# A GELU between two matmuls: half of a loaded in whole rows and turned ahead of the first matmuls

## The chip, the cores and the metric

The kernel runs on one core of a Trainium2 chip. The metric is the device time in microseconds (us) of one execution. Five engines work side by side: TensorE (PE in the profile; its weight loads are PEld), VectorE (DVE), ScalarE (ACT), GpSimd (POOL) and SyncE (SP). SP, ACT and GpSimd can issue transfers (DMAs), and 16 DMA engines carry them out.

## The reference

```
m, k, n, p = 1024, 1024, 2048, 1024        # a: m x k, b: k x n, c: n x p, all float32
h = np.matmul(a, b)
h = 0.5 * h * (1 + np.tanh(np.sqrt(2 / np.pi) * (h + 0.044715 * h ** 3)))
return np.matmul(h, c).astype(np.float32)
```

## The kernel before

The first product is computed transposed: TensorE holds a 128 x 128 tile of b as its weight and streams 512 columns of the transposed a (aT) past it, so that a PSUM bank collects a 128 x 512 tile of h transposed over eight k-tiles. ScalarE applies the GELU on the way out of PSUM. M is split into two halves of 512 rows (aT[0] and aT[1]), N into 16 tiles of 128. [...]a must be cast and turned (transposed on TensorE against an identity, then copied out of PSUM), and b must be cast.

The instructions of each engine run in the order in which the program issues them; the schedule is written by hand, and the framework adds only the waits. The stages are these.

1. **The opening** (lines 74 to 117), the stage that the diff touches. load_a0 brings the first 512 rows of a as columns of k: two pieces with one k-tile each, then three with two, each piece covering all four row tiles. load_b0 brings slice k of b: 128 rows and the first W0 = 768 columns (six N-tiles). All these loads stand in one queue, SP's, a's pieces alternating with b's slices. Ten matmuls on zeros (line 96) run meanwhile. Then, for each k, VectorE casts the piece of a (line 107), TensorE turns its four row tiles (line 110), VectorE copies the result to aT[0] (line 111), ScalarE casts b's slice in two halves (line 113), and TensorE does the six matmuls of the slice before (mm0, line 102). Six PSUM banks (ps) collect six tiles of h.
2. **The gate** (line 91): GpSimd copies one element of slice 5 of b, so that it waits for that slice to land. Behind it in GpSimd's queue stand all later loads, which cast on the way: columns 768 to 1279 of b (b_lo, line 126), then the rest of b (b_hi), the other 512 rows of a (line 155, turned at line 162) and c (line 188).
3. **Four more N-tiles** for the first half of M (line 134), then the remaining six (mm1, line 143), then all sixteen for the second half.
4. **The second product** (prod, line 246), which forms h times c from seven products of half size and sums that VectorE makes. The results leave by SP. The last tile is cut into two column ranges, each with its own eight matmuls, its sum on VectorE (line 316) and its store.

Pools that matter: astage has four buffers of 4 KB per partition (pieces of a before the cast), b0stage eight (slices of b), abf four (pieces of a after the cast), ppool six PSUM banks, tpool two.

Of the kernel before, what the change touches and what calls it, by code (L numbers as in the profile page):

```python
# [9 lines left out]
F32 = mybir.dt.float32  # L10
BF16 = mybir.dt.bfloat16
F32R = mybir.dt.float32r
SUB = mybir.AluOpType.subtract
ADD = mybir.AluOpType.add
AF = mybir.ActivationFunctionType
# [4 lines left out]
def kernel(ctx, tc, a, b, c, out):  # L20
    nc = tc.nc
    M, K = a.shape
    _, N = b.shape
    _, P = c.shape
    KT = K // 128
    NT = N // 128
    MT = M // 128
    H = 512
    N0 = 6
    W0 = N0 * 128  # L30
# [3 lines left out]
    av = a.rearrange("(mt p) k -> p mt k", p=128)  # L34
    bv = b.rearrange("(kt p) n -> p kt n", p=128)
# [5 lines left out]
    astage = ctx.enter_context(tc.tile_pool(name="astage", bufs=4))  # L41
    abf = ctx.enter_context(tc.tile_pool(name="abf", bufs=4))
# [3 lines left out]
    tpool = ctx.enter_context(tc.tile_pool(name="tpool", bufs=2, space=PSUM))  # L46

    warm = consts.tile([128, H], BF16, name="warm")
    nc.vector.memset(warm, 0.0)
    ident = consts.tile([128, 128], BF16, name="ident")  # L50
# [3 lines left out]
    aT = [keep.tile([128, KT, H], BF16, name=f"aT{h}", tag=f"A{h}") for h in range(2)]  # L54
    WB = W0 + W1
    b_lo = keep.tile([128, KT, WB], BF16, name="b_lo", tag="B0")
# [7 lines left out]
    def bt(k, t):  # L64
        return bcols(k, 1, t * 128, 128)[:, 0, :]
# [5 lines left out]

    a_st, b_st = {}, {}

    def load_a0(k, n):
        st = astage.tile([128, 4, 256], F32, name="a_st")
        nc.sync.dma_start(out=st[:, :, 0:n * 128], in_=av[:, 0:4, ds(k * 128, n * 128)])  # L76
        for i in range(n):
            a_st[k + i] = st[:, :, ts(i, 128)]

    def load_b0(k):  # L80
        st = b0stage.tile([128, W0], F32, name="b0_st")
        nc.sync.dma_start(out=st, in_=bv[:, k, 0:W0])  # L82
        b_st[k] = st

    gate = consts.tile([128, 1], F32, name="gate")
    for k, n in ((0, 1), (1, 1), (2, 2), (4, 2), (6, 2)):
        load_a0(k, n)
        for i in range(n):
            load_b0(k + i)

    nc.gpsimd.tensor_copy(gate, b_st[5][:, 0:1])  # L91
    g = consts.tile([128, 1], F32, name="g")
    nc.scalar.activation(g, warm[:, 0:1], AF.Gelu_apprx_tanh)
    wps = tpool.tile([128, H], F32, name="pt")
    for _ in range(10):
        nc.tensor.matmul(wps, warm[:, 0:128], warm, start=True, stop=True)

    ps = [ppool.tile([128, H], F32, name="ps") for _ in range(N0)]

    def mm0(k):  # L100
        for t in range(N0):
            nc.tensor.matmul(ps[t], bt(k, t), aT[0][:, k, :],  # L102
                             start=(k == 0), stop=(k == KT - 1))

    for k in range(KT):
        ab = abf.tile([128, 4, 128], BF16, name="ab")
        nc.vector.tensor_copy(ab, a_st[k])  # L107
        pt = tpool.tile([128, H], BF16, name="pt")
        for j in range(4):
            nc.tensor.transpose(pt[:, ts(j, 128)], ab[:, j, :], ident)  # L110
        nc.vector.tensor_copy(aT[0][:, k, :], pt)
        for i in range(2):
            nc.scalar.activation(b_lo[:, k, ts(i, W0 // 2)], b_st[k][:, ts(i, W0 // 2)], AF.Copy)  # L113
        if k > 0:
            mm0(k - 1)
    mm0(KT - 1)

    def gelu(t, h, p):
        nc.scalar.activation(hq[h][t // NH][:, t % NH, :], p, AF.Gelu_apprx_tanh)  # L119
# [5 lines left out]
    def load_b(k0, kn, n0, w):  # L125
        nc.gpsimd.dma_start(out=bcols(k0, kn, n0, w), in_=bv[:, k0:k0 + kn, ds(n0, w)])

    ps = [(tpool if t < 2 else ppool).tile([128, H], F32, name="pt" if t < 2 else "ps")
          for t in range(N1)]
    for k in range(0, KT, 4):  # L130
        load_b(k, 4, W0, W1)
        for i in range(4):
            for t in range(N1):
                nc.tensor.matmul(ps[t], bt(k + i, N0 + t), aT[0][:, k + i, :],  # L134
                                 start=(k + i == 0), stop=(k + i == KT - 1))
# [17 lines left out]
    for j in range(4):  # L153
        st = abf.tile([128, K], BF16, name="ab1")
# [27 lines left out]
    c21 = keep.tile([128, NH, H], BF16, name="c21")  # L182
# [25 lines left out]
    for t in range(NT):  # L208
# [10 lines left out]
        if WB // 128 <= t < WB // 128 + 4:  # L219
            i = t - WB // 128  # L220
# [20 lines left out]
    def bank(w=H):  # L241
        return ppool.tile([128, w], F32, name="ps", padded_shape=[128, H])

    def prod(p, lhs, rhs, j, q=slice(0, H)):
        for t in range(NH):
            nc.tensor.matmul(p, lhs(t)[:, ts(j, 128)], rhs(t)[:, q],  # L246
                             start=(t == 0), stop=(t == NH - 1))

    def whole(x):
        return lambda t: x[:, t, :]  # L250
# [10 lines left out]
    def new_out():  # L261
        return opool.tile([128, H], F32, name="ot")

    def store(ot, m, q0, w=H):
        nc.sync.dma_start(out=out[ts(m, 128), ds(q0, w)], in_=ot[:, 0:w])

    def combine(m, q, p, u, op=ADD, swap=False):
        ot = new_out()
        nc.vector.tensor_tensor(ot, u if swap else p, p if swap else u, op=op)  # L269
        store(ot, m, q * H)  # L270
# [5 lines left out]
    for j in R:  # L276
        p = bank()
        prod(p, whole(h11), whole(c11), j)
        nc.scalar.activation(u2[j], p, AF.Copy)  # L279
    for j in range(3):  # L280
        p = bank()
# [3 lines left out]
    last_keep = opool.tile([128, H], F32, name="lk", bufs=1)  # L285
    nc.gpsimd.tensor_copy(last_keep, last)  # L286
    for j in R:
        p = bank()
        prod(p, halves(s2), ones(t2), j)
        nc.vector.tensor_tensor(u2[j], p, u2[j], op=ADD)  # L290
    for j in R:
        p = bank()
# [3 lines left out]
    for j in R:  # L296
        p = bank()
# [5 lines left out]
    for j in R:  # L303
        p = bank()
        prod(p, halves(s2), whole(c22), j)
        combine(j, 1, p, u2[j])
    for j in R:
        p = bank()
        prod(p, whole(h22), ones(t2), j)
        combine(4 + j, 0, p, u3[:, j, :], op=SUB, swap=True)  # L310
    for q in range(2):
        w = H // 2
        p = bank(w)
        prod(p, whole(h12), whole(c21), 3, q=ds(q * w, w))
        ot = new_out()
        nc.vector.tensor_tensor(ot[:, 0:w], p, last_keep[:, ds(q * w, w)], op=ADD)  # L316
        store(ot, 3, q * w, w)

# [1 line left out]
_INS = ['a', 'b', 'c']  # L320
# [26 lines left out]
```

## Time and profile before

| what | us |
|---|---|
| median of 13 runs | 125.14 |
| lowest and highest of them | 124.48, 126.1 |
| the profiled execution's own time | 125.14 |
| its span, first to last instruction | 123.4 |
| PE busy | 114.9 (93%) |
| DVE busy | 65.2 (53%) |
| ACT busy | 29.6 (24%) |
| POOL busy | 21.3 (17%) |

All times of instructions are counted from the start of the span. Matmuls are pipelined: one of 512 columns is listed with some 379 ns, but at the full clock the next starts 216 ns after it, so starts are more useful than durations. The granted clock of TensorE is given as a share of full speed. A DMA's time "to landing" counts from the start of its issue to the arrival of all of it.

### The profile page before, as it was taken

The numbers are of one execution on the slowest core, as the hardware profiler recorded it, in microseconds if no ns is written. First come the engines' busy times: TensorE is split into PE (matmuls) and PEld (weight loads), VectorE is DVE, ScalarE is ACT, GpSimd is POOL, SyncE is SP. The second block draws the span as 40 slices with busy tenths as digits, with TensorE's granted clock in tenths as the row PEclk, the third lists the DMA queues.
The fourth block names the chain that finished last, engine by engine and source line by source line (L and its number), as shares of the span: only waits on it lengthen the run. The fifth ranks groups of instructions, "written<-read, shape, count | busy, mean of one in ns | idle before, by whom it ended". The sixth has DMA issues, their size and how long they took to land.

```text
span 123.4 us, 1443 instructions
## 1 busy us (share of the span) xinstructions
PE 114.9 (93%) x562; PEld 67.1 (54%) x562; DVE 65.2 (53%) x94; ACT 29.6 (24%) x54; POOL 21.3 (17%) x26
## 2 busy tenths in 40 slices
PE   6639989999998999999999999999999999999990
PEld 2224444344455544444444444468888888888860
DVE  0223543000005300006999999999769999964440
ACT  4044545805432132333323332100000000000000
POOL 2000099133440220000000000896000000000000
PEclk9977999999999999999999999999999999999999
DMA  3899999999999999995000000000600022354433
GB/s 105 180 351 381 380 318 192 205 201 203 212 205 207 319 396 234 206 206 96 1 3 0 5 0 0 0 0 5 250 0 0 5 85 106 149 189 151 170 141 114
DMA packets 14213, 18.43 MB, mean 149 GB/s; under 512 B 768, under 2 KB 9728, under 8 KB 14208
## 3 DMA queue, kind: packets, MB, share of 16 engines
q0 software_dynamic: 7968, 8.91, 39.2%
q1 hardware_dynamic: 6240, 9.44, 22.0%
q8 instruction: 4, 0.07, 0.2%
q14 instruction: 1, 0.01, 0.0%
HBM read 20.97 MB, written 4.19 MB: 204 GB/s over the span
## 4 chain that ended last, share of the span: by engine, by line
PE 78%; DMA 13%; SPq 4%; DVE 1%; issue 1%; POOL 0%
PE ps L246 41%; PE ps L143 31%; DMA b_st<-in_b_dram 7%; DMA b_lo<-in_b_dram 5%; PE pt L134 3%; PE ps L134 3%; SPq L82 3%; SPq L76 2%; PE pt L162 1%; DVE aT L163 1%; DVE ot L316 0%; POOL gate L91 0%
## 5 line engine op out<-in xcount | busy, mean ns | idle before, releaser
L119 ACT ACTIVATE h<-ps 128x512 fp32r<-128x512 f32 (+1 forms) x30 | 17.3, 601 | 27.5 <-PE ps L143 26.3
L143 PE MATMUL ps<-aT,b_hi 128*128 128x512 bf16 x96 | 21.4, 379 | 0.0
L143 PE MATMUL ps<-aT,b_lo 128*128 128x512 bf16 x80 | 17.4, 379 | 0.0
L143 PEld LDWEIGHTS <-b_hi 128*128 128x128 bf16 x96 | 9.3, 98 | 10.9
L246 PE MATMUL ps<-t,s 128*128 128x512 f32 x64 | 15.0, 392 | 0.0
L246 PE MATMUL ps<-t,h 128*128 128x512 f32 x64 | 14.8, 389 | 0.0
L246 PE MATMUL ps<-c,h 128*128 128x512 bf16 (+1 forms) x72 | 14.2, 355 | 0.0
L286 POOL COPY lk<-u 128x512 f32<-128x512 f32 x1 | 7.8, 7828 | 33.4 <-ACT u L279 33.4
L246 PEld LDWEIGHTS ps<-t,s 128*128 128x128 f32 x64 | 12.0, 188 | 2.6
L246 PEld LDWEIGHTS ps<-t,h 128*128 128x128 f32 x64 | 12.0, 188 | 2.5
L143 PEld LDWEIGHTS <-b_lo 128*128 128x128 bf16 x80 | 7.8, 98 | 9.4
L200 DVE TENSOR_TENSOR t<-c,c 128x1024 fp32r<-128x1024 bf16 x4 | 4.7, 1222 | 15.6 <-DMA c<-in_c_dram 15.4
L102 PE MATMUL ps<-aT,b_lo 128*128 128x512 bf16 x48 | 12.7, 408 | 0.0
L163 DVE COPY aT<-pt 128x1024 bf16<-128x1024 bf16 x4 | 2.7, 689 | 18.5 <-PE pt L162 18.4
L246 PEld LDWEIGHTS <-h 128*128 128x128 bf16 x72 | 7.0, 98 | 7.0 <-issue 0.3
L113 ACT ACTIVATE b_lo<-b_st 128x384 bf16<-128x384 f32 x16 | 7.5, 515 | 10.2 <-DMA b_st<-in_b_dram 10.1
L188 POOL DMA_DIRECT2D c<-in_c_dram x8 | 5.9, 743 | 12.3 <-PE ps L143 6.2
L269 DVE TENSOR_TENSOR ot<-ps,u 128x512 f32<-128x512 f32 x11 | 7.3, 683 | 1.1 <-PE ps L246 1.1
L246 PE MATMUL ps<-c,s 128*128 128x512 f32 x32 | 7.4, 389 | 0.0
L102 PEld LDWEIGHTS <-b_lo 128*128 128x128 bf16 x48 | 4.7, 105 | 4.6 <-issue 0.8
L107 DVE CAST ab<-a_st 128x512 bf16<-128x512 f32 x8 | 3.7, 461 | 6.3 <-DMA a_st<-in_a_dram 6.3
L246 PEld LDWEIGHTS ps<-c,s 128*128 128x128 f32 x32 | 6.0, 188 | 1.2
(37 smaller groups left out, 89.8 us busy)
## 6 DMA issues: line engine op xcount, KB each, us to landing
out_dram<-ot SPq DMA_DIRECT2D x15, 256.0 KB, 2.0
b_st<-in_b_dram SPq DMA_DIRECT2D x8, 384.0 KB, 8.4
c<-in_c_dram POOLq DMA_DIRECT2D x6, 512.0 KB, 14.9
c<-in_c_dram POOLq DMA_DIRECT2D x2, 1024.0 KB, 15.3
a_st<-in_a_dram SPq DMA_DIRECT2D x3, 512.0 KB, 8.5
b_hi<-in_b_dram POOLq DMA_DIRECT2D x4, 384.0 KB, 11.4
b_lo<-in_b_dram POOLq DMA_DIRECT2D x2, 512.0 KB, 7.5
ab<-in_a_dram POOLq DMA_DIRECT2D x4, 256.0 KB, 13.8
```

The costliest lines, as they stand in the source:

```text
L82: nc.sync.dma_start(out=st, in_=bv[:, k, 0:W0])
L102: nc.tensor.matmul(ps[t], bt(k, t), aT[0][:, k, :], start=(k == 0), stop=(k == KT - 1))
L113: nc.scalar.activation(b_lo[:, k, ts(i, W0 // 2)], b_st[k][:, ts(i, W0 // 2)], AF.Copy)
L119: nc.scalar.activation(hq[h][t // NH][:, t % NH, :], p, AF.Gelu_apprx_tanh)
L134: nc.tensor.matmul(ps[t], bt(k + i, N0 + t), aT[0][:, k + i, :], start=(k + i == 0), stop=(k + i == KT - 1))
L143: nc.tensor.matmul(p, bt(k, t), aT[h][:, k, :], start=(k == 0), stop=(k == KT - 1))
L163: nc.vector.tensor_copy(aT[1][:, :, ts(j, 128)], pt)
L188: nc.gpsimd.dma_start(out=dst[:, t:t + 4, :], in_=cv[:, r * NH + t:r * NH + t + 4, ts(q, H)])
L200: nc.vector.tensor_tensor(t1[i], c12[:, ts(i, 2), :], c11[:, ts(i, 2), :], op=SUB)
L246: nc.tensor.matmul(p, lhs(t)[:, ts(j, 128)], rhs(t)[:, q], start=(t == 0), stop=(t == NH - 1))
L269: nc.vector.tensor_tensor(ot, u if swap else p, p if swap else u, op=op)
L286: nc.gpsimd.tensor_copy(last_keep, last)
```

## The change

The opening is ordered anew, in six points.

- The 512 rows of a come in whole rows instead of columns of k: row tiles 0 and 1 in one load each (1024 columns), row tiles 2 and 3 in two loads each (columns 0 to 511, and 512 to 1023).
- Slice 0 of b is issued by ScalarE, ahead of everything else on that engine; all other loads of the opening stay with SP, in the order a's row tiles 0, 1, the left halves of 2 and 3, slice 1 of b, the right halves of 2 and 3, slices 2 to 7 of b.
- Six groups of four transposes (the left halves of all row tiles and the right halves of 0 and 1) come ahead of the first matmul of mm0; the other two stand in the middle of the matmuls of k = 1 and k = 2. Casts of a and copies out of PSUM are shared between VectorE and ScalarE, and each slice of b is cast half by VectorE and half by ScalarE.
- The matmuls on zeros become eight at the start, three after the second group of transposes and three after the fourth; they write to a bank of ppool.
- GpSimd's gate reads slice 4 of b instead of slice 5.
- At the end of the kernel, the last tile is cut into 384 and 128 columns instead of 256 and 256.

```diff
-    def load_a0(k, n):
-        st = astage.tile([128, 4, 256], F32, name="a_st")
-        nc.sync.dma_start(out=st[:, :, 0:n * 128], in_=av[:, 0:4, ds(k * 128, n * 128)])
-        for i in range(n):
-            a_st[k + i] = st[:, :, ts(i, 128)]
-
-    def load_b0(k):
+    def load_a0(mt, k0, n):
+        st = astage.tile([128, n * 128], F32, name="a_st")
+        nc.sync.dma_start(out=st, in_=av[:, mt, ds(k0 * 128, n * 128)])
+        a_st[mt, k0] = st
+
+    def load_b0(k, queue=nc.sync):
         st = b0stage.tile([128, W0], F32, name="b0_st")
-        nc.sync.dma_start(out=st, in_=bv[:, k, 0:W0])
+        queue.dma_start(out=st, in_=bv[:, k, 0:W0])
         b_st[k] = st
...
-    for k, n in ((0, 1), (1, 1), (2, 2), (4, 2), (6, 2)):
-        load_a0(k, n)
-        for i in range(n):
-            load_b0(k + i)
-
-    nc.gpsimd.tensor_copy(gate, b_st[5][:, 0:1])
+    load_b0(0, nc.scalar)
+    load_a0(0, 0, KT)
+    load_a0(1, 0, KT)
+    load_a0(2, 0, 4)
+    load_a0(3, 0, 4)
+    load_b0(1)
+    load_a0(2, 4, 4)
+    load_a0(3, 4, 4)
+    for k in range(2, KT):
+        load_b0(k)
+
+    nc.gpsimd.tensor_copy(gate, b_st[4][:, 0:1])
...
-    wps = tpool.tile([128, H], F32, name="pt")
-    for _ in range(10):
-        nc.tensor.matmul(wps, warm[:, 0:128], warm, start=True, stop=True)
...
+    def warm_up(n):
+        for _ in range(n):
+            nc.tensor.matmul(ps[N0 - 1], warm[:, 0:128], warm, start=True, stop=True)
+
+    warm_up(8)
+
+    def half(mt, k0, off=0):
+        src = a_st[mt, k0 - off][:, ds(off * 128, 512)]
+        ab = abf.tile([128, 512], BF16, name="ab")
+        if off and mt < 2 or off and mt == 3:
+            nc.scalar.activation(ab, src, AF.Copy)
+        else:
+            nc.vector.tensor_copy(ab, src)
+        return ab
+
+    def turn0(mt, k0, ab):
+        pt = tpool.tile([128, 4, 128], BF16, name="pt")
+        for k in range(4):
+            nc.tensor.transpose(pt[:, k, :], ab[:, ts(k, 128)], ident)
+        dst = aT[0][:, k0:k0 + 4, ts(mt, 128)]
+        if k0 == 0:
+            nc.vector.tensor_copy(dst, pt)
+        else:
+            nc.scalar.activation(dst, pt, AF.Copy)
+
+    HW = W0 // 2
+
+    def cast_b0(k):
+        nc.vector.tensor_copy(b_lo[:, k, 0:HW], b_st[k][:, 0:HW])
+        nc.scalar.activation(b_lo[:, k, HW:W0], b_st[k][:, HW:W0], AF.Copy)
+
+    steps = [(0, 0, 0), (0, 4, 4), (1, 0, 0), (1, 4, 4), (2, 0, 0), (3, 0, 0)]
+    ab = [half(*x) for x in steps[:2]]
+    for i, x in enumerate(steps):
+        if i % 2 == 0 and i + 2 < len(steps):
+            ab += [half(*y) for y in steps[i + 2:i + 4]]
+        turn0(x[0], x[1], ab[i])
+        if i == 1:
+            cast_b0(0)
+        if i in (1, 3):
+            warm_up(3)
+    cast_b0(1)
+    for k in range(KT):
+        if k == 1:
+            ab = [half(2, 4), half(3, 4)]
+        if k > 0 and k + 1 < KT:
+            cast_b0(k + 1)
         for t in range(N0):
             nc.tensor.matmul(ps[t], bt(k, t), aT[0][:, k, :],
                              start=(k == 0), stop=(k == KT - 1))
-
-    for k in range(KT):
-        ab = abf.tile([128, 4, 128], BF16, name="ab")
-        nc.vector.tensor_copy(ab, a_st[k])
-        pt = tpool.tile([128, H], BF16, name="pt")
-        for j in range(4):
-            nc.tensor.transpose(pt[:, ts(j, 128)], ab[:, j, :], ident)
-        nc.vector.tensor_copy(aT[0][:, k, :], pt)
-        for i in range(2):
-            nc.scalar.activation(b_lo[:, k, ts(i, W0 // 2)], b_st[k][:, ts(i, W0 // 2)], AF.Copy)
-        if k > 0:
-            mm0(k - 1)
-    mm0(KT - 1)
+            if k in (1, 2) and t == 2:
+                turn0(k + 1, 4, ab[k - 1])
...
-    for q in range(2):
-        w = H // 2
+    for q0, w in ((0, 384), (384, 128)):
         p = bank(w)
-        prod(p, whole(h12), whole(c21), 3, q=ds(q * w, w))
+        prod(p, whole(h12), whole(c21), 3, q=ds(q0, w))
         ot = new_out()
-        nc.vector.tensor_tensor(ot[:, 0:w], p, last_keep[:, ds(q * w, w)], op=ADD)
-        store(ot, 3, q * w, w)
+        nc.vector.tensor_tensor(ot[:, 0:w], p, last_keep[:, ds(q0, w)], op=ADD)
+        store(ot, 3, q0, w)
```

More of the change, by code (lines that the diff above doesn't have):

```diff
@@ L92 @@
+    load_a0(2, 0, 4)
[6 more added lines that the diff above has]
+    nc.gpsimd.tensor_copy(gate, b_st[4][:, 0:1])
     g = consts.tile([128, 1], F32, name="g")
     nc.scalar.activation(g, warm[:, 0:1], AF.Gelu_apprx_tanh)
-    wps = tpool.tile([128, H], F32, name="pt")
-    for _ in range(10):
-        nc.tensor.matmul(wps, warm[:, 0:128], warm, start=True, stop=True)
     ps = [ppool.tile([128, H], F32, name="ps") for _ in range(N0)]
-    def mm0(k):
+    def warm_up(n):
+        for _ in range(n):
+            nc.tensor.matmul(ps[N0 - 1], warm[:, 0:128], warm, start=True, stop=True)
```

## The prediction

> **What bounds the kernel now.** I read the chain of waits in order of time first, since it tells which stage sets the end.
>
> ```profile
> 6.50 9.11 DMA b_st<-in_b_dram
> 15.61 0.05 issue
> 15.66 0.12 POOL gate L91
> 15.78 6.70 DMA b_lo<-in_b_dram
> 22.48 0.05 issue
> 22.53 0.61 PE pt L134 x2
> ...
> 39.15 0.02 issue
> 39.17 0.70 DVE aT L163
> 39.88 0.04 issue
> 39.92 0.61 PE pt L162 x8
> 40.53 29.35 PE ps L143 x136
> 69.88 50.14 PE ps L246 x232
> 120.02 0.02 issue
> 120.05 0.42 DVE ot L316
> ```
>
> The columns are start, length, what. Up to 22.53 the chain is loads: slice 5 of b, the gate on GpSimd, the next columns of b. From 22.53 to 120.02 it is TensorE, save a 0.5 us hole before 39.92, which the timeline ends with the third transposed tile's copy. So I split the time into four: 22.53 (call it **D**, the first matmul of line 134) + 97.5 of dense TensorE + 3.4 of tail to the span's 123.4 + 1.74 outside the span = 125.14, which is also the median of the 13 runs. The opening can only move D; the last edit can only move the tail.
>
> Then the opening itself, microsecond by microsecond (busy time of PE, PEld, DVE, ACT, POOL, then granted clock, share of the DMA engines, GB/s):
>
> ```profile
> 2.00:3.00 1.00, 1.00 (x4) 0.42 (x3) 0.00 (x0) 0.22 (x2) 0.00 (x0) 1.00 0.92 278
> 3.00:4.00 1.00, 1.00 (x4) 0.33 (x3) 0.43 (x1) 0.00 (x0) 0.00 (x0) 1.00 0.95 191
> 4.00:5.00 1.00, 1.00 (x8) 0.50 (x6) 0.00 (x0) 0.00 (x0) 0.00 (x0) 1.00 0.72 148
> 5.00:6.00 1.00, 0.12 (x3) 0.00 (x0) 0.42 (x1) 0.00 (x0) 0.00 (x0) 1.00 0.77 199
> ...
> 8.00:9.00 1.00, 0.92 (x6) 0.65 (x7) 0.30 (x2) 0.34 (x1) 0.00 (x0) 0.50 1.08 393
> 9.00:10.00 1.00, 1.00 (x4) 0.36 (x3) 0.15 (x1) 0.60 (x2) 0.00 (x0) 0.50 1.08 413
> ```
>
> Two losses stand here. The loads move 148 to 199 GB/s from 3 to 6 us, against some 385 afterwards. And the clock is 0.50 when the first real matmuls run: they start 0.427 us apart from 8.48 to 10.62, later ones 0.216, so six cost 1.3 us extra. After 11 us TensorE waits little: 0.2 us before 14.18, 0.5 before 17.72, and 0.46 from the end of the 48 matmuls of line 102 (19.47 + 12 x 0.216 = 22.06) to D, which the new columns of b (landed 22.48) end. The last slice of the first b block was issued at 10.15 and took 8.9 us: 19.05.
>
> **What the Trainium skill says.** "TensorE: Matmul & The Clock Gate", Part 1: the clock is half by default, goes full after a window of about 3.4 us of activity, and falls back after an idle one. The trace agrees: full from 4.09 us, half at 8.08 after 3.0 us of idle, full from 10.95. "DMA: Bandwidth & Descriptors", Issuing engines are not separate DMA queues: a second issuing engine saves issue time only, the 16 engines are shared. Before uses one hardware queue, so no trace shows it. The same page, Specifications, names 512 B as enough for line rate; this trace differs: packets of 512 B took about 26 ns (16 engines: 315 GB/s), of 3072 B about 125 ns (393). "ScalarE: Activation LUTs", What ACT_TABLE_LOAD costs: an ACTIVATE takes 186 ns + 0.833 per element, so 506 for 384 elements; the trace has 515.
>
> **The change, part by part.**
>
> *Loads.* The same 5.24 MB. The half of a was 5 loads of 512 B and 1 KB pieces (about 46 ns each, 356 GB/s); it becomes 6 loads of 2 and 4 KB pieces. At 393 GB/s that saves (0.52/315 + 1.57/356) - 2.10/393 = 0.7 us of transfer. Issues: SP loses one of b (0.49) to ACT, whose table load (1.28) and dummy gelu then start about 0.5 later; ACT's first use was at 6.43 and is now near 5.5, so this is covered. SP's row loads queued sixth and seventh (mt 2 and 3, right halves) need a staging buffer back, the pool having four: they wait for both casts of mt 0 and of mt 1. All slices of b from 2 on are queued behind them. When they wait, 1.97 to 2.6 MB are issued ahead, 5 us of transfer, and the casts come 0.6 us after those rows land; I cost it at nothing, and at up to 0.5 if a cast is late.
>
> *When the transposes are done.* The last piece needed before the first matmul is row tile 3, left half. Ahead of it and in it lie 0.39 (b slice 0) + 2 x 0.52 + 2 x 0.26 = 1.97 MB. **Lower bound:** first bytes at 2.0 us, 385 GB/s, so 5.1 us, and 0.8 from the bytes to the landing (before: 5.24 MB were through at 18.2, the last landed at 19.05): 7.9. **Upper bound:** the pace of before, whose rows by microsecond sum to 1.97 MB at 9.3, with the 0.8: 10.1. In that slow stretch single 3072-byte packets took 300 to 800 ns while the engines' share was 0.72 to 0.77: engines stood idle with one queue in order. Two queues and long pieces should fill some of it. I take 8.5.
>
> From that landing DVE has, in order: cast (0.43), the copy of T(1,0) that stands behind it (0.42), then TensorE's four transposes (0.39), two copies (0.42 each), and five hops of about 0.04: 2.3 us. The first matmul is at **S = 10.8** (10.2 to 12.4). Before it was 8.48: the new order puts the first matmul some 2.3 us later, and must win that back by having no waits after it.
>
> *TensorE from S on.* 48 matmuls x 0.216 = 10.37, plus two groups of four transposes at 0.056 = 0.45; six groups that stood between matmuls have moved ahead of S. No wait is expected between: a slice of b lands each 1.0 us, and a slice is used each 1.3. Slice 1 lands at 8.5 + 1.0, a's right halves 1.4 later, slice 2 at 11.9, slice 7 at 17 to 18; their use would be at S + 2.6 = 13.4 for slice 2 and S + 9.5 = 20.3 for slice 7. The halves of a cast cost 0.51 on ACT and about 0.33 on DVE (0.43 x 384/512); even at the 0.65 that a DVE cast took beside GpSimd's issues at 18.49 they fit in 1.3. Before, ACT spent 1.03 per slice and was no bound, so halving gains nothing by itself. So **D = 10.8 + 10.8 = 21.6**, a gain of 0.9 on 22.53; at the two bounds 21.0 (gain 1.5) and 23.2 (loss 0.7).
>
> *The gate.* Slice 4 instead of 5 lands 1.0 sooner in the order: 8.5 + 1.0 + 1.4 + 3.0 = 13.9. Before, 6.8 us passed from gate to the columns' landing, with two and a half slices' worth still queued; now three. 13.9 + 6.8 + 0.2 = 20.9, which is 0.7 ahead of D. Later loads on GpSimd shift 1.7 earlier against 0.9 for their users, so the wait of before does not return: the four row tiles of a landed 1.5 to 2.2 ahead of their turns. If that cover were gone, D would follow the landing one for one.
>
> *Clock.* Warm-up goes from ten to eight matmuls plus two groups of three. Between 4.6 and S TensorE is busy 6 x 4 transposes and 6 matmuls, 2.6 us of 6.2 at full clock; the window of before that led to half clock had about 1.1 busy of 3.4. If half clock falls on S, it costs up to 1.7 (half of 3.4), or nothing. I take nothing for the likeliest.
>
> *Tail.* 384 + 128 columns for 256 + 256. TensorE: 8 x 0.163 + 8 x 0.056 = 1.75, as before. DVE: 689 ns for 512 columns and 424 for 256 give 1.035 ns per column: 0.56 for 384, starting at 118.09 + 1.30 + 0.2 = 119.59, to 120.15; then 0.29, to 120.48, where before ended at 120.47. SP's stores start at least 0.6 apart (119.0 and 119.62), so the second starts at 120.8, not 120.5, and moves 64 KB less, some 0.25 us. Net 0; bounds -0.3 and +0.3.
>
> Sum: 21.6 + 97.5 + 3.4 + 1.74 = **124.2**.
>
> **Rivals.** *Slower: the start-up rate is a property of the first microseconds, not of the small pieces.* For it: 3072-byte packets of b were themselves slow from 3 to 6 us, while 512-byte packets of a ran at 26 ns. Then all four row tiles, which now must land before any matmul, come at 10.1, S is 12.4, D 23.2, the time 125.9. It decides from a landing of row tile 3 at 9.4. Against it: idle engines in that stretch. *Half clock at S.* For it: 1.1 busy of 3.4 sufficed to lose the clock before, and the new gaps wait for rows. Against: if the clock falls early, the slow transposes and warm-ups fill the next window. At 1.2 it makes 125.4. *Full-rate loads from the start:* landing 7.9, 123.6. *The columns behind the gate bound:* if sharing with slices 5 to 7 costs 1.5 more than before, D is 22.4 and the time 125.0: the whole edit would be hidden.
>
> **How the numbers follow.** Loads: full rate 0.28, partly slow 0.47, as slow as before 0.25. Half clock at S with 0.8 or more: 0.25 in each; the gate takes another 0.05 from the gains. About 0.5%, or 0.6 us, is what a measurement of this kernel can tell from no change. Faster by more: 0.75 x 0.75 less 0.04 = 0.52. Within: 0.23, nearly all the cold or gated part of the gains. Slower: 0.25. The likeliest case alone spans 123.7 to 124.8. The range takes the full-rate case with the tail's good end, 123.1, to the slow start-up, 126.0.
>
> **What would show it.** In the profile after: row tile 3's cast at 8.5 (9.4 or more: the rival); first matmul of the four-column-tile loop (line 134 before) at 21.6; the 48 matmuls 0.216 apart from the first, with clock 1.00; no DMA wait ahead of them but row tiles; GpSimd's gate near 13.9; GB/s over 250 from 3 to 6 us. I am wrong on the mechanism if matmuls after S wait for b or a cast, or if the 97.5 us of dense work changes by over 0.3.

## The result, and the profile after

The change makes the kernel slower: 126.64 us, the median of 11 runs (125.86 to 127.95), against 125.03 for the kernel before in the same comparison. The ratio is 1.0125, with a 95% interval of 1.0101 to 1.0150. The prediction was 124.2, faster; the measured time lies above its range. Now and then an execution runs slower at a lower granted clock; the ratios leave such executions out, and in two experiments below (128.23 and 139.01 us) the profiled execution was one of them.

The chain of waits in order of time of the changed kernel (start, length, what) shows the same division into an opening and dense TensorE work, with a later seam.

```profile
1.17 6.24 DMA a_st<-in_a_dram
7.40 0.02 issue
7.43 0.64 ACT ab L111
8.07 0.02 issue
8.08 0.33 SPq L76
8.41 0.05 issue
8.46 7.20 DMA b_st<-in_b_dram
15.67 0.02 issue
15.69 0.37 DVE b_lo L129
16.06 0.05 issue
16.11 0.82 PE ps L149 x3
...
17.15 7.12 PE ps L149 x33
24.27 0.49 PE pt L170 x2
...
71.51 49.73 PE ps L282 x224
121.24 0.02 issue
121.27 0.06 DVE ot L351
```

Read it backwards. From 16.11 TensorE is dense. What released it there is VectorE's cast of a slice of b, and behind that stands a load of 7.20 us that was issued only at 8.46. SP issued it so late because the load ahead of it (line 76, a right half of a, issued at 8.08) needed a staging buffer, which came free with ScalarE's cast of 7.43, and that cast waited for a row tile of a. So the path runs through a cast, SP's queue and a load; the link between them is the staging buffer.

The timeline puts D, the first matmul behind the 48 of the opening (line 170 now), at 24.16, where before had 22.53. From D to the first matmul of the last tile it is 95.6 us in both (24.16 to 119.75; 22.53 to 118.09). All of the loss, 1.63 us of D for 1.6 us of span (125.0 against 123.4), lies in the opening.

The table by microsecond (busy time of PE, PEld, DVE, ACT, POOL, then clock, share of the DMA engines, GB/s) answers to the one shown of before:

```profile
2.00:3.00 1.00, 1.00 (x4) 0.43 (x3) 0.00 (x0) 0.67 (x2) 0.00 (x0) 1.00 0.55 161
3.00:4.00 1.00, 1.00 (x4) 0.33 (x3) 0.00 (x0) 0.00 (x0) 0.00 (x0) 1.00 0.82 288
4.00:5.00 1.00, 0.78 (x2) 0.00 (x0) 0.00 (x0) 0.00 (x0) 0.00 (x0) 1.00 0.88 324
5.00:6.00 1.00, 0.00 (x0) 0.00 (x0) 0.09 (x1) 0.09 (x1) 0.00 (x0) 1.00 1.04 371
...
9.00:10.00 1.00, 1.00 (x8) 0.65 (x6) 0.62 (x2) 0.41 (x1) 0.00 (x0) 1.00 0.90 301
10.00:11.00 1.00, 1.00 (x10) 0.60 (x9) 0.03 (x1) 0.60 (x2) 0.00 (x0) 1.00 0.68 174
11.00:12.00 1.00, 0.38 (x5) 0.14 (x2) 1.00 (x4) 0.00 (x0) 0.00 (x0) 1.00 0.53 161
12.00:13.00 1.00, 1.00 (x6) 0.48 (x5) 0.67 (x2) 0.00 (x0) 0.00 (x0) 1.00 1.00 181
13.00:14.00 1.00, 1.00 (x10) 0.57 (x8) 0.00 (x0) 0.00 (x0) 0.00 (x0) 1.00 0.86 215
```

The slow stretch of before, 148 to 199 GB/s from 3 to 6 us, is gone: 288 to 371, though from 2 to 3 us the loads are slower than before (161 against 278). A new slow stretch stands from 10 to 14 us. SP issued nothing from 3.45 to 6.56 us, and again from 6.89 to 8.08; the waits of SP say for what it waited (us in total, times, longest):

```profile
SPq L76 <- DVE ab L113: 3.9, 2, 2.9
```

The timeline of TensorE alone (start, length, what, what ended the idle time before it) shows the stretch from 6 to 17 us:

```profile
6.39 1.03 PE L119 MATMUL pt<-ident,ab 128*128 128x128 bf16 x8 [1.61 <-DVE ab L113]
7.22 1.49 PE L103 MATMUL ps<-warm 128*128 128x512 bf16 x3
8.50 1.06 PE L119 MATMUL pt<-ident,ab 128*128 128x128 bf16 x8
9.35 1.36 PE L103 MATMUL ps<-warm 128*128 128x512 bf16 x3
10.55 0.61 PE L119 MATMUL pt<-ident,ab 128*128 128x128 bf16 x8
11.78 2.10 PE L149 MATMUL ps<-aT,b_lo 128*128 128x512 bf16 x9 [0.62 <-DVE aT L122]
...
13.95 0.81 PE L149 MATMUL ps<-aT,b_lo 128*128 128x512 bf16 x3
16.11 0.82 PE L149 MATMUL ps<-aT,b_lo 128*128 128x512 bf16 x3 [1.35 <-DVE b_lo L129]
```

Line 119 are transposes, line 103 the matmuls on zeros, line 149 the 48 real ones. Two things are to be seen. Until 10.55 the clock is at half: eight transposes take 1.03 us, not 0.61, and the matmuls on zeros start 0.427 apart, those from 1.19 on too. (The clock column has 1.00 there; the starts show otherwise.) And TensorE waits from the end of the row at 13.95 to 16.11 for slice 2 of b.

### The profile page after: what moved, and what is told of

Read it like the earlier page. It is cut to its first block, busy times and chain, and to the rows that moved or that the text cites. A ratio compares the mean times of both kernels' runs of the same rounds, so it can differ in the third digit from the quotient of the medians.

```text
span 125.0 us, 1451 instructions
## 1 busy us (share of the span) xinstructions
PE 116.6 (93%) x566; PEld 67.9 (54%) x566; DVE 64.7 (52%) x96; ACT 29.3 (23%) x52; POOL 22.3 (18%) x26
## 3 DMA queue, kind: packets, MB, share of 16 engines
HBM read 20.97 MB, written 4.19 MB: 201 GB/s over the span
## 4 chain that ended last, share of the span: by engine, by line
PE 84%; DMA 11%; DVE 1%; issue 1%; SPq 1%; ACT 1%; DVEq 0%
PE ps L282 40%; PE ps L179 30%; PE ps L149 6%; DMA b_st<-in_b_dram 6%; DMA a_st<-in_a_dram 5%; PE pt L170 3%; PE ps L170 3%; PE pt L198 1%; SPq L76 1%; DVE aT L199 1%; ACT ab L111 1%; DVE b_lo L129 0%; DVEq L377 0%; PE pt L119 0%; DVE ot L351 0%
## 5 line engine op out<-in xcount | busy, mean ns | idle before, releaser
L179 PE MATMUL ps<-aT,b_lo 128*128 128x512 bf16 x80 | 17.4, 379 | 0.0
L179 PEld LDWEIGHTS <-b_hi 128*128 128x128 bf16 x96 | 9.3, 98 | 10.8
L322 POOL COPY lk<-u 128x512 f32<-128x512 f32 x1 | 8.5, 8499 | 33.2 <-ACT u L315 33.2
L282 PE MATMUL ps<-c,h 128*128 128x512 bf16 (+2 forms) x72 | 14.2, 355 | 0.0
L149 PE MATMUL ps<-aT,b_lo 128*128 128x512 bf16 x48 | 11.0, 379 | 2.0 <-DVE b_lo L129 1.4
L103 PE MATMUL ps<-warm 128*128 128x512 bf16 x14 | 6.4, 623 | 1.2 <-DVE warm L49 1.2
L129 DVE CAST b_lo<-b_st 128x384 bf16<-128x384 f32 x8 | 2.9, 368 | 5.9 <-DMA b_st<-in_b_dram 5.9
```

Source lines behind the costliest of these rows:

```text
L103: nc.tensor.matmul(ps[N0 - 1], warm[:, 0:128], warm, start=True, stop=True)
L129: nc.vector.tensor_copy(b_lo[:, k, 0:HW], b_st[k][:, 0:HW])
L149: nc.tensor.matmul(ps[t], bt(k, t), aT[0][:, k, :], start=(k == 0), stop=(k == KT - 1))
L179: nc.tensor.matmul(p, bt(k, t), aT[h][:, k, :], start=(k == 0), stop=(k == KT - 1))
L282: nc.tensor.matmul(p, lhs(t)[:, ts(j, 128)], rhs(t)[:, q], start=(t == 0), stop=(t == NH - 1))
```

## The experiments

My theory after this: **SP's wait for a staging buffer, with every later slice of b behind it, is the loss; the half clock ahead of the first matmul is a second one, hidden behind it.** The rival: loads run slowly whenever SP issues a burst of slices of b, whatever it waited for.

### Spare staging memory

The two right halves go to memory that the second half of h takes over only later.

```diff
+    spare = [keep.tile([128, 512], F32, name=f"sp{g}", tag=f"h1{g}") for g in range(2)]
...
-        st = astage.tile([128, n * 128], F32, name="a_st")
+        st = spare[mt - 2] if k0 else astage.tile([128, n * 128], F32, name="a_st")
```

> The changed kernel, with the two right halves of row tiles 2 and 3 staged in memory that is free until later, so that SP's loads no longer wait for a staging buffer. Theory (the loss is SP's wait for a buffer, with all slices of b queued behind it): slice 2 lands near 12 us instead of 15.67, the loads keep above 300 GB/s from 9 to 14 us, no matmul of the first 48 waits for slice 2, the first column-tile matmul behind them starts at about 22.6 (11.8 + 10.8) instead of 24.16, and the time falls by 1.3 to 1.6 us, to that of the kernel before. Rival (loads are slow whenever SP issues a burst of slices of b, whatever it waited for): 150 to 220 GB/s for some 3 us remain, only earlier, and the time falls by less than 0.7.

Measured: 125.12, ratio to before 1.0016 (0.9993 to 1.0039), so 1.1% or 1.4 us below the change. Slice 2 landed at 12.05, the last slice at 16.93 (change: 20.48; before: 19.01), the 48 matmuls had no wait for a slice and D was 22.49. The loads from 9 to 14 us (same columns as above):

```profile
9.00:14.00 5.00, 4.38 (x27) 2.30 (x27) 2.83 (x9) 1.53 (x3) 0.00 (x0) 1.00 1.03 407
```

For comparison, the change:

```profile
9.00:14.00 5.00, 4.38 (x31) 2.44 (x29) 2.32 (x7) 1.01 (x2) 0.00 (x0) 1.00 0.79 206
```

The theory holds in each number. The rival's stretch of 3 us at 150 to 220 GB/s did not come. A milder one did: from 8 to 9 us the loads ran at 281 GB/s (309 in the run below), where the change had 407. No matmul waited for it, and no run says what makes it.

### Two slices ahead of the waiting halves

Here the buffers stay four and SP still waits; slices 2 and 3 are issued first. The right halves are cast and turned one k later, behind the casts of that slice.

```diff
     load_b0(1)
+    load_b0(2)
+    load_b0(3)
     load_a0(2, 4, 4)
     load_a0(3, 4, 4)
-    for k in range(2, KT):
+    for k in range(4, KT):
```

> The changed kernel with four staging buffers as it has them, but SP issues slices 2 and 3 of b ahead of the two right halves that wait for a buffer; their transposes stand one k later. Theory (slices behind the buffer wait): slices 2 and 3 are issued before 6.5 us, land by 11.5 and 12.5, the matmuls do not wait for them, the 48 matmuls end near 22.5 and the time falls by 1.3 to 1.6 us against the change. Rival (slow bursts): moving the burst of issues forward slows the rows of a that are in flight, the last left half lands after 9.5 instead of 8.74, and less than 0.7 us is won.

Measured: 124.85, ratio 1.0013 (0.9988 to 1.0038), from the same comparison as the one above, so again 1.4 us below the change. The last left half landed at 8.68, slices 2 and 3 by 11.70. SP issued the right halves at 6.43 and 8.01, as late as in the change, and four slices between 8.38 and 10.4, and yet:

```profile
9.00:14.00 5.00, 4.27 (x25) 2.10 (x25) 3.06 (x9) 2.11 (x4) 0.00 (x0) 1.00 1.02 397
```

So neither the wait alone nor the burst behind it costs. What differs is how much was issued ahead of it. From the sizes of the loads and the packets moved until then: when SP went on to the slices, 1.53 MB were still to be moved here (3.8 us at 407 GB/s), and 0.69 MB in the change (1.7 us). That too little was left in the queue is the reading that fits both runs; neither varies the amount by itself.

This profile had one more difference, which is not of the edit's making. The clock was at full under the transposes, after the same eight matmuls on zeros:

```profile
1.20 3.28 PE L105 MATMUL ps<-warm 128*128 128x512 bf16 x8 [1.20 <-DVE warm L49]
6.26 0.62 PE L121 MATMUL pt<-ident,ab 128*128 128x128 bf16 x8 [1.79 <-DVE ab L115]
```

The change needed 3.60 us for those eight matmuls and 1.03 for the transposes. So this profile's first matmul, at 10.84, and its D, 21.84, are better than the edit alone explains. The 1.4 us are from the times of 14 runs, not from this profile.

### The gate and the tail alone, on the kernel before

```diff
-    nc.gpsimd.tensor_copy(gate, b_st[5][:, 0:1])
+    nc.gpsimd.tensor_copy(gate, b_st[4][:, 0:1])
```

> The kernel before with one edit: GpSimd's gate reads slice 4 of b instead of slice 5. Theory: the gate opens 1.0 us sooner, the next columns of b land some 0.5 to 1.0 us before 22.48, the wait of 0.46 us ahead of them goes, and the time falls by 0.2 to 0.45 us. Rival (the loads of GpSimd take bandwidth from slices 6 and 7 of b): the last matmuls of the first block wait instead and the time stays or grows by up to 0.5.

Measured: 124.65, ratio 0.9985 (0.9962 to 1.0008). In its profile b_lo landed at 21.46 and D was 22.06, so the wait did go; the time does not tell it from no change.

> The kernel before with one edit: the last tile is cut 384 + 128 instead of 256 + 256. The prediction's sum: net 0, within 0.3 us either way: the last sum on VectorE ends at the same time and the last store is shorter but issued no sooner.

Measured: 124.86, ratio 1.0010 (0.9988 to 1.0031). Net zero, as summed.

### Twelve matmuls on zeros instead of eight

First with the spare staging memory, then on the change as it is.

```diff
-    warm_up(8)
+    warm_up(12)
```

> The changed kernel with the spare staging memory (no wait of SP for a buffer), and twelve matmuls on zeros at the start instead of eight, so that TensorE has no gap of 2 us ahead of the first transposes. Theory (what is left of the prediction's miss is the half clock under the transposes and the inner matmuls on zeros): transposes start 0.056 apart, the first real matmul moves from 11.7 to about 10.8, the matmuls behind the first 48 start at 21.6 to 21.9 instead of 22.5, and the time is 0.5 to 0.9 us below the kernel with spare staging alone, so below the kernel before. Rival (the next columns of b, behind the gate, are the bound as soon as the 48 matmuls end sooner): under 0.3 us is won and TensorE waits for b_lo ahead of the column tiles.

> The changed kernel as it is (four staging buffers), only with twelve matmuls on zeros at the start. Theory (in the change as it is, the late slice 2 sets the end, not the first matmul): the first matmul comes up to 0.9 us sooner and waits that much longer for slice 2 at 15.7, and the time moves by less than 0.3 us. Rival (half clock is a cost of its own in the change): 0.5 to 0.9 us are won.

With spare memory: 124.45, ratio 0.9972 (0.9959 to 0.9985), the first version that beats the kernel before. TensorE's timeline in it:

```profile
6.48 0.62 PE L119 MATMUL pt<-ident,ab 128*128 128x128 bf16 x8 [0.87 <-DVE ab L113]
6.94 0.81 PE L103 MATMUL ps<-warm 128*128 128x512 bf16 x3
8.32 0.74 PE L119 MATMUL pt<-ident,ab 128*128 128x128 bf16 x8 [0.57 <-DVE aT L122]
8.89 0.81 PE L103 MATMUL ps<-warm 128*128 128x512 bf16 x3
9.76 0.61 PE L119 MATMUL pt<-ident,ab 128*128 128x128 bf16 x8
10.99 2.10 PE L149 MATMUL ps<-aT,b_lo 128*128 128x512 bf16 x8 [0.62 <-DVE aT L122]
```

Against the change, the second group of matmuls on zeros ends 1.0 us sooner (9.70; 10.71), and the first real matmul comes at 10.99 instead of 11.78, although the last left half landed no sooner (8.83; 8.74). D is 21.80. Since the profile above had the full clock with eight, what twelve do is best read from the spread of the times: with spare memory 124.23 to 125.80 over 14 runs with eight, 124.27 to 124.67 over 22 with twelve. That fits eight leaving the clock to chance, and twelve not. It stays a reading, since the gate run below, with twelve as well, spreads from 124.19 to 125.50.

On the change as it is: 126.64, ratio 1.0117 (1.0078 to 1.0156), where the change itself has 1.0125: no difference. In the profile (of an execution of 128.23 us, so only what stands ahead of slice 2 is used) the first matmul came at 10.85, slice 2 at 15.43, and the wait for it grew (us in total, times, longest; the change had 1.35):

```profile
PE ps L149 <- DVE b_lo L129: 2.1, 1, 2.1
```

So in the change the half clock costs nothing, since slice 2 ends last; it becomes a cost when the buffer wait is gone.

### No matmuls on zeros between the transposes

```diff
-        if i in (1, 3):
-            warm_up(3)
```

> The changed kernel with the spare staging memory, without the two groups of three matmuls on zeros between the transposes. If those groups, at half clock 1.3 us each, only delay the transposes: the first real matmul comes 0.4 to 0.9 us sooner. If they keep the clock up: the first matmuls run 0.427 apart for 1 to 3 us and lose 0.5 to 1.5 us. I expect both, with a net between -0.3 and +0.8 us against the kernel with spare staging alone.

Measured, with spare memory: 126.71, ratio 1.0146 (1.0108 to 1.0183), 1.6 us above the kernel with spare memory alone, twice the largest loss expected. The first matmul came at 11.12, 0.6 sooner, and the clock stayed at half:

```profile
11.12 4.00 PE L147 MATMUL ps<-aT,b_lo 128*128 128x512 bf16 x9 [0.52 <-DVE aT L122]
...
15.35 1.93 PE L147 MATMUL ps<-aT,b_lo 128*128 128x512 bf16 x5
...
17.33 7.29 PE L147 MATMUL ps<-aT,b_lo 128*128 128x512 bf16 x33
```

Nine matmuls take 4.00 us here and 2.10 in the kernel with spare memory alone. There the clock is at half too, but comes up at 10.5 us, just behind the second group on zeros; here it comes up at about 16.4. D was 24.46 (22.49).

### Slice 0 of b, by which queue

On SP, in the kernel with spare memory:

```diff
-    load_b0(0, nc.scalar)
+    load_b0(0)
```

> The changed kernel with the spare staging memory, and slice 0 of b issued by SP ahead of a instead of by ScalarE. If two queues fill the slow start of the loads: the stretch from 3 to 6 us falls from some 310 to 360 GB/s towards the 150 to 200 of the kernel before, the last left half lands at 9.5 to 10, and 0.7 to 1.3 us are lost. If the queue is only a matter of issue time: row tile 0 is issued 0.4 later, and 0 to 0.5 us are lost.

Measured: 125.66, ratio 1.0087 (1.0053 to 1.0121). That is above the kernel with spare memory alone by 0.54 us if one goes by the medians and by 0.9 us if one goes by the ratios, so it does not tell the two expectations apart; the last left half landed at 9.24 instead of 8.63. The rate from 2 to 6 us was 289 GB/s against 291, so "a second queue fills the slow start" is not what this run shows.

By ScalarE and first, in the kernel before:

```diff
+    load_b0(0, nc.scalar)
     for k, n in ((0, 1), (1, 1), (2, 2), (4, 2), (6, 2)):
         load_a0(k, n)
         for i in range(n):
-            load_b0(k + i)
+            if k + i:
+                load_b0(k + i)
```

> The kernel before with one edit: slice 0 of b is issued by ScalarE, first. If the second queue is what lifts the slow start of the loads: 250 GB/s and more from 3 to 6 us, the last slice lands near 18 instead of 19.0, the wait of 0.46 us for the next columns of b goes, and 0.3 to 0.5 us are won. If the long pieces are what lifts it: 150 to 200 GB/s stay, and the time moves by less than 0.2.

Measured: 124.38, ratio 0.9951 (0.9921 to 0.9981). The last slice landed at 18.11 instead of 19.01, D was 21.16, and the first loads ran faster (this run, then before):

```profile
2.00:6.00 4.00, 3.64 (x9) 1.06 (x7) 0.06 (x1) 1.04 (x3) 0.00 (x0) 1.00 0.94 254
...
2.00:6.00 4.00, 3.12 (x13) 1.26 (x11) 0.85 (x2) 0.22 (x2) 0.00 (x0) 1.00 0.84 204
```

This one line of the change, alone, wins 0.6 us (0.2 to 1.0 by the interval). The four profiles do not split the gain of the loads into two clean parts. The last slice landed at 19.01 before, at 18.11 with the queue alone, at 17.43 with the rows and no second queue, and at 16.93 with both: the queue is worth 0.9 us beside the columns and 0.5 beside the rows (the last two have spare memory and the new order as well).

### With loads and clock in order: gate, casts, copies

All three start from spare memory and twelve matmuls on zeros (0.9972).

```diff
-    nc.gpsimd.tensor_copy(gate, b_st[4][:, 0:1])
+    nc.gpsimd.tensor_copy(gate, b_st[5][:, 0:1])
```

> The kernel with spare staging memory and twelve matmuls on zeros at the start, with GpSimd's gate on slice 5 again. The gate opens 1.0 us later; the next columns of b, which landed at 20.0 with TensorE coming to them at 21.8, land at about 20.9 to 21.2. Theory (the gate is covered): no change, within 0.2 us. Rival: a wait of up to 0.5 us for b_lo returns.

Measured: 124.40, ratio 0.9968 (0.9948 to 0.9988). The columns landed at 20.97, TensorE came to them at 21.58. The gate's slice is covered.

```diff
-        nc.vector.tensor_copy(b_lo[:, k, 0:HW], b_st[k][:, 0:HW])
+        nc.scalar.activation(b_lo[:, k, 0:HW], b_st[k][:, 0:HW], AF.Copy)
```

> The kernel with spare staging memory and twelve matmuls on zeros at the start, with both halves of each slice of b cast by ScalarE, as in the kernel before. ScalarE then needs 1.03 us per slice, where TensorE needs 1.3. Theory (the halving gains little by itself): 0 to 0.3 us are lost, from casts that stand ahead of copies of transposes on ScalarE. Rival (ScalarE becomes the bound): more than 0.5 us are lost, and matmuls wait for casts.

Measured: 124.21, ratio 0.9936 (0.9915 to 0.9956). Neither loss came; halving the casts of b wins nothing, and may cost 0.2 us (against the gate run of the same comparison, by the medians).

```diff
-        if k0 == 0:
+        if k0 == 0 and mt != 2:
...
-            ab += [half(*y) for y in steps[i + 2:i + 4]]
+            ab += [half(*y) for y in steps[i + 2:i + 4 - i // 2]]
         turn0(x[0], x[1], ab[i])
+        if i == 2:
+            ab.append(half(3, 0))
...
-            warm_up(3)
+            warm_up(3 if i == 1 else 2)
```

> The kernel with spare staging memory and twelve matmuls on zeros at the start, with three further edits: VectorE copies the transposed left half of row tile 1 ahead of its cast of row tile 3, ScalarE copies that of row tile 2, and the second inner group of matmuls on zeros has two instead of three. Theory (with loads and clock in order, the first matmul's start sets the end one for one): it moves from 11.0 to about 10.5, the column tiles behind it start at 21.3 instead of 21.8, and 0.3 to 0.5 us are won against the kernel without these edits. Rival (the columns behind the gate, or the clock, take it back): the time moves by less than 0.15.

Measured: 124.00, ratio 0.9917 (0.9885 to 0.9948): 0.4 us below the gate run of the same comparison, inside the expectation, and the fastest version. Its profiled execution took 139.01 us, so the earlier starts that the expectation names were not seen; only the times are shown.

## Why the prediction was wrong

- **The step that failed: "SP's row loads queued sixth and seventh ... need a staging buffer back ... I cost it at nothing, and at up to 0.5 if a cast is late."** The wait was foreseen, its price was not: 1.5 us. The casts were not late: they began within 0.1 us of the landings of row tiles 0 and 1 (5.88 and 7.40). The step counted the bytes issued in all ("1.97 to 2.6 MB", by the order of the loads 2.36 and 2.62, "5 us of transfer"), and not those still to be moved when SP could go on. The right half issued at 6.56 still had 0.95 MB ahead of it and moved at full pace (84 ns a piece). The one issued at 8.08 had 0.59 MB ahead, 1.5 us, and from about 9.4 the loads slowed. Slice 2 was issued at 8.46; its first packets moved at about 11.0, 2.5 us later, and the loads ran at 161 to 215 GB/s until 14. It landed at 15.67, not at 11.9. TensorE was through with slice 1 at 14.60 and waited until 16.11. Spare memory, or two slices issued ahead of the wait, takes 1.4 us back.
- **The landing of row tile 3, 8.5: right (8.74).** The rival, that all of the slow start would repeat, did not happen: 10.1 was its number. Of the two reasons given, the long pieces seem to bear more: with them and without the second queue the landing was 9.24.
- **S, the first matmul, 10.8: wrong by 1.0 (11.78).** A quarter is the landing, the rest the clock: three matmuls on zeros at 0.427 hold TensorE until 10.55. "I take nothing for the likeliest" was the step. The half clock did not fall on S; it lay on the work ahead of S, which the prediction named ("the slow transposes and warm-ups") and did not price. With the clock up S is 10.99.
- **10.8 us from S to D without waits: right where slices arrive.** With spare memory and the clock up it is 21.80 - 10.99 = 10.81.
- **The miss adds up:** 1.0 (S) + 1.5 (slice 2) + 0.05 = 2.55, and D is 24.16 against 21.6.
- **The gate opened at 17.67, not at 13.9,** since it waits for slice 4; the columns landed at 24.12 just as the 48 matmuls ended, so they cost nothing in this profile, but by chance rather than by the 0.7 us of the sum. The one slice of the gate, which the prediction did not cost by itself, shows no effect alone (0.9985) or undone (0.9968 against 0.9972).
- **Tail and dense part: right**, zero and unchanged. Two terms of the tail's sum were too large and cancel. SP's last stores stood 0.42 us apart (121.85 and 122.28), not at least 0.6, so the last began 0.12 us later than before, counted from the last tile's first matmul, and not 0.3. It landed after 1.75 us instead of 1.85, which saves 0.1 and not 0.25. Two readings were slightly off and bear on nothing: the hole before 39.92 ends with the copy of the second turned tile (39.17 to 39.87), not of the third, and the last slice landed at 19.01, not at 19.05.
- **The sum of the opening was near for another kernel:** with the buffer wait and the half clock removed, D is 21.80 where 21.6 was predicted. The time is then 124.45 where 124.2 was predicted; but the kernel before had 124.81 in that comparison, so the gain is 0.35 us (0.2 to 0.5 by the interval) and not 0.9. The profile of before, with D at 22.53, is of an execution of 125.14 us, above that median.

## What to carry to other kernels

When a load queue is reordered, look for the first load that must wait for a buffer, and estimate how much of what was issued ahead is still to be moved when the wait ends. Here that was 1.7 us of work, and the first data of the next load came 2.5 us after its issue; all that was queued behind started late and slowly. Loads without a wait go ahead of those with one. And a warm-up that is cut short may leave the clock at half: the price is paid by the work that follows, and shows only once nothing else ends later.

## What the runs showed of the hardware

- **Loads that found little ahead of them in the queue ran slowly.** In the change, pieces of 3072 bytes that take 121 ns in flow took 160 to 270 ns on average from 11 to 14 us, single ones over 1 us. From 3 to 5.5 us of the kernel before they took 240 to 285 ns, single ones up to 0.8 us. With 1.5 MB kept ahead through the same SP waits the window had 397 GB/s instead of 206. A milder dip (281 and 309 GB/s from 8 to 9 us) came with 1.4 MB and more queued, so little work ahead is not the only cause. Why the packets are slow is open.
- **Length of the pieces.** Pieces of 4096 bytes took 159 ns and of 2048 bytes 84 ns: with 16 engines 412 and 390 GB/s, against 315 for the 512-byte pieces before.
- **Which queue issues the first slice: no more than the issue time is shown.** "DMA: Bandwidth & Descriptors" of the Trainium skill, Issuing engines are not separate DMA queues, says that a second issuing engine saves only issue time. An issue is 0.4 to 0.5 us here; moving it won 0.6 us in the kernel before and lost 0.5 to 0.9 us when undone, with intervals that include 0.5. In the one pair of profiles the rate from 2 to 6 us differed (254 against 204 GB/s), in the other it did not (291 against 289).
- **Matmuls between transposes brought the clock up.** With two groups of three on zeros it was full from 10.5 us; without them it stayed at half until about 16.4, through 28 transposes and some twelve matmuls since 6.36.
- **The same warm-up can end at either clock.** Eight matmuls on zeros from 1.2 us on left the transposes at half clock in two profiles (the change, and with spare memory: 1.03 us for eight) and at full in one (0.62).
